# First stage of a two-layer streaming encoder: the third token block is scaled, shifted and split part by part

## The chip, the cores and the metric

The kernel runs on one core of a Trainium2 chip. The metric is the device time of one execution in microseconds (us), as the median over several executions. The core has a matrix engine (PE, with its weight loads listed as PEld), a vector engine (DVE), a scalar engine (ACT), a general engine (POOL) and a queue engine (SP) that issues most of the loads. Each engine works through its own queue of instructions in the order in which the program holds them; semaphores tie them together.

## The reference, cut to what matters

2,048 prompt tokens and 128 sample tokens (8 requests of 16) pass through two layers. Each layer normalises, modulates by a scale and a shift that depend on the request, mixes, and adds the result back. The change touches the beginning of the first layer only:

```
def rms_norm(x, g):
    xf = x.astype(F32)
    y = xf * lax.rsqrt(jnp.mean(xf * xf, axis=-1, keepdims=True) + EPS)
    return (y * g.astype(F32)).astype(x.dtype)
...
        h = rms_norm(x, norm_g[i]) * (1.0 + scale) + shift
...
    proj = h @ w_in
    u, z = jnp.split(proj, 2, axis=-1)
```

So `h = x * r * gs + shift`, where `r` is one number per token (the reciprocal root), `gs = norm_g * (1 + scale)` is one number per feature (and request), and `shift` likewise. All 2,048 prompt tokens share one request; the sample tokens have eight.

## The kernel before

**Layout.** The 2,176 tokens are cut into eight blocks, `j` = 0 to 7, of 272 tokens: 256 of the prompt (`NPC`) and 16 of the samples. A block is a tile `x` of 128 partitions by 8 by 272: feature `128 k + p` lies in part `k` on partition `p`. The program numbers blocks from 0, so the **third block** is `j` = 2; its tile is called `x2` here and shows as `x` in the profile.

**Products.** The products are done in three parts for accuracy. A block is split into a high part `hh` (what the matrix engine's 32-bit format holds) and a low part `hl` (the rest), each as two tiles of four parts (`_0` for k = 0 to 3, `_1` for k = 4 to 7); weights are split likewise (`wuh`, `wul`). `mm3` (L148 to L154) issues three matmuls for each k: high by high (L151), high weight by low block (L152), low weight by high block (L153). A column block `cb` of 128 outputs takes 24 matmuls into one accumulator tile `pd`, a token block takes 8 column blocks, 192 matmuls. From block 1 on four accumulator buffers serve `pd` in turn; ACT copies each finished one to `ev` and stores it to `u_d`.

**The first stage.** A loop over the blocks `j` does, in this order of the code: four column blocks; then the preparation of block `j + 1` (modulate and split), the load of `x` for block `j + 2`; then four more column blocks, and at the end (cb = 7) the normalisation `norm_x` of block `j + 2` (squares on ACT, sums on DVE, a sum over the partitions by two matmuls `ms`, a root on ACT, a reciprocal on DVE, and a multiply of the whole block by `r` on DVE). Block 0 and block 1 have code of their own ahead of the loop: block 0 is prepared k by k, and block 1 by `second_block`, part by part. Blocks 2 to 7 are prepared by `apply_mod` (L283), in three turns: eight activations on ACT that apply `gs` and the shift to the already normalised block in place, one after another (L291); a copy of four parts at a time to `hh` on ACT, and a subtraction on DVE for `hl` (`split_x`, L229). The modulated block is also stored to `h0_d[j]`, from where a later stage reads it again.

**What else runs on the engines there.** Small tables of the state-space mixer are made on DVE and POOL (`transitions`, `step_factors`, `s5_tables`, `rot_factors`, `rot_table`: the rows with `gk`, `sm`, `low`, `high`, `q`, `ca`, `cat`, `sp`, `tw`), and from block 2 on PE also does the products of `ada_steps` (`ada<-wa,cs`), whose weights SP loads between the blocks. The buffers of `x` are three, so the load of `x5` waits until `x2` is read and stored.

**What sets the order.** Each engine is wrapped in a class with a flag `ordered`. While it is set, that engine's instructions keep the order in which the code writes them (in the profile they all show the wrapper's line, L70). While it is not set, a scheduler chooses their places, and they show the line of the code that issues them. PE is ordered while `j` = 1; DVE and ACT are ordered while blocks 0 and 1 are prepared and while `x2` is normalised, and not after that.

**The later stages**, which the change does not touch: the scan of the state-space mixer with the product for `z` between its parts, the gating product (`pg`), the output product (`po`), the second layer's input product with its convolution (`pc`, `pz`), the sample tokens, and sixteen chunks of the delta rule with the last product (`epo`) beside them.

Of the kernel before, what the change touches and what calls it, by code (L numbers as in the profile page):

```python
# [10 lines left out]
F32 = mybir.dt.float32  # L11
F32R = mybir.dt.float32r
# [6 lines left out]
P = 128  # L19
# [3 lines left out]
NCH = 272  # L23
# [31 lines left out]
def kernel(ctx: ExitStack, tc: tile.TileContext, I, O, upto="Z"):  # L55
    nc = tc.nc
# [18 lines left out]
    T, V, S, G, SY = (Engine(e) for e in (nc.tensor, nc.vector, nc.scalar, nc.gpsimd, nc.sync))  # L75
# [10 lines left out]
    h0_d = [dr.tile([P, KC, NCH], F32, name=f"h0_d{i}") for i in range(8)]  # L86
# [133 lines left out]
    hp = pab.enter_context(tc.tile_pool(reuse_waits="tile", name="hp", bufs=4))  # L220
# [11 lines left out]
    with ExitStack() as pa:  # L232
        xp = pa.enter_context(tc.tile_pool(reuse_waits="tile", name="xp", bufs=3))
        sst = pa.enter_context(tc.tile_pool(reuse_waits="tile", name="sst", bufs=1))
# [12 lines left out]
        def norm_sq(xt, sqs=None, acc=None, part=range(2)):  # L247
            acc = sp1.tile([P, 2, NCH], F32, tag="acc", name="acc") if acc is None else acc
            for hf in part:
                sq = sqs[:, 4 * hf:4 * hf + 4] if sqs else sp1.tile([P, 4, NCH], F32, tag="sq", name="sq")  # L250
                xh = xt[:, 4 * hf:4 * hf + 4]
                S.activation(sq, xh, AF.Square)
                V.tensor_add(sq[:, 0:2], sq[:, 0:2], sq[:, 2:4])
                V.tensor_add(acc[:, hf], sq[:, 0], sq[:, 1])
            return acc
# [9 lines left out]
        def norm_r(acc, r=None, fold=False):  # L265
            ps = psn.tile([P, NCH], F32, tag="ms", name="ms")
            if fold:
                V.tensor_add(acc[:, 0], acc[:, 0], acc[:, 1])
            for hf in range(1 if fold else 2):
                T.matmul(ps, lhsT=onesd, rhs=acc[:, hf], start=(hf == 0), stop=(fold or hf == 1))  # L270
            r = sp1.tile([P, NCH], F32, tag="r", name="r") if r is None else r
            S.activation(r, ps, AF.Sqrt, bias=epst)
            V.reciprocal(r, r)
            return r
# [5 lines left out]
        def norm_x(xt, fold=False):  # L280
            return norm_mul(xt, norm_r(norm_sq(xt), fold=fold))

        def apply_mod(j, xt):  # L283
            xs = xt[:, :, NPC:NCH].rearrange("p k (q h) -> p k q h", h=2)
            V.tensor_mul(xs, xs, bc(gs0[:, :, 1:9], 3, 2))
            V.tensor_add(xs, xs, bc(modT[:, 0:8, 1:9], 3, 2))
            hl = []
            for hf in range(2):
                for k in range(4 * hf, 4 * hf + 4):
                    xk = xt[:, k, 0:NPC]  # L290
                    S.activation(xk, xk, AF.Identity, scale=gs0[:, k, 0:1], bias=modT[:, k, 0:1])  # L291
                hl.append(split_x(j, xt[:, 4 * hf:4 * hf + 4], hf))
            (h0, l0), (h1, l1) = hl
            if j < 7:
                nc.scalar.dma_start(h0_d[j], xt)
            return h0 + h1, l0 + l1

        def second_block(xt, r, copies):
            xs = xt[:, :, NPC:NCH].rearrange("p k (q h) -> p k q h", h=2)
            V.tensor_mul(xs, xs, bc(r[:, NPC:NCH].rearrange("p (q h) -> p q h", h=2), 1, KC))  # L300
            V.tensor_mul(xs, xs, bc(gs0[:, :, 1:9], 3, 2))
            V.tensor_add(xs, xs, bc(modT[:, 0:8, 1:9], 3, 2))
            a, b = ([hp.tile([P, 4, NCH], F32R, tag=t, name=f"{t}1_{hf}") for hf in range(2)] for t in ("hh", "hl"))
            for hf in range(2):
                for i in range(4):
                    k = 4 * hf + i
                    xk = xt[:, k, 0:NPC]
                    V.scalar_tensor_tensor(xk, r[:, 0:NPC], gs0[:, k, 0:1], xk, op0=ALU.mult, op1=ALU.mult)
                    S.activation(a[hf][:, i, 0:NPC], xk, AF.Identity, bias=modT[:, k, 0:1])
                S.copy(a[hf][:, :, NPC:NCH], xt[:, 4 * hf:4 * hf + 4, NPC:NCH])  # L310
                for cb in copies[hf]:
                    first_copy(cb)
                for i in range(4):
                    k = 4 * hf + i
                    V.scalar_tensor_tensor(b[hf][:, i, 0:NPC], xt[:, k, 0:NPC], modT[:, k, 0:1],
                                           a[hf][:, i, 0:NPC].bitcast(F32), op0=ALU.add, op1=ALU.subtract)
                V.tensor_sub(b[hf][:, :, NPC:NCH], xt[:, 4 * hf:4 * hf + 4, NPC:NCH],
                             a[hf][:, :, NPC:NCH].bitcast(F32))
            for k in range(KC):
                xk = xt[:, k, 0:NPC]  # L320
                S.activation(xk, xk, AF.Identity, bias=modT[:, k, 0:1])
            nc.scalar.dma_start(h0_d[1], xt)
            return [ks(t[0], 4) + ks(t[1], 4) for t in (a, b)]

        SY.ordered = True
# [74 lines left out]
        wt, raws = load_mod(0), [load_raw(0), load_raw(1)]  # L400
        T.ordered = V.ordered = S.ordered = True
        xsq = xp.tile([P, KC, NCH], F32, tag="x", name="xsq")
        r0 = norm_r(norm_sq(xcur, xsq), sst.tile([P, NCH], F32, name="r0"))
        W = 32
        sm = sst.tile([P, 11 * W], F32, name="sm")
        sml = [sm[:, i * W:(i + 1) * W] for i in range(11)]
# [1 line left out]
        for k in range(KC):  # L408
# [5 lines left out]
            if k == 6:  # L414
                xt1 = load_x(1)[0]
# [29 lines left out]
        for cb in range(6, 8):  # L445
            pd0 += [psd.tile([P, NCH], F32, tag="d", name=f"pd0_{cb}")]
            mm3(pd0[cb], ks(wu_hi[cb]), ks(wu_lo[cb]), *hcur)
        hnext = second_block(xt1, r1, ((2, 3), (4, 5)))
        first_copy(6)
        first_copy(7)  # L450
        after = [V.last]
# [169 lines left out]
        for j in range(8):  # L621
            hh, hl = hcur
            T.ordered = j == 1
            for cb in range(8):
                if cb == 4:
                    if j < 7:
                        hcur = apply_mod(j + 1, xnext) if j else hnext
                    V.ordered = S.ordered = j == 0
                    if j < 6:
                        xn, xl = load_x(j + 2)  # L630
                        if j == 0:
                            xnext = norm_x(xn)
                    V.ordered = S.ordered = False
                    SY.ordered = False
                    with later([i_] if j else after):
                        for part in TABLES.get(j, ()):
                            s5_tables(part)
                        if j == 1:
                            rot_factors()
                        for i in range(max(0, 3 * j - 3), min(3 * j, 16)):  # L640
                            rot_table(i)
                if j > 0:
                    ps = psd4.tile([P, NCH], F32, tag="d", name=f"pd{j}_{cb}")
                    i_ = mm3(ps, ks(wu_hi[cb]), ks(wu_lo[cb]), hh, hl)
                    store_u(j, cb, ps)
                if cb == 7 and 0 < j < 6:
                    xnext = norm_x(xn)
                if j > 1 and cb % 3 == 1:
                    with later([xl, i_]):
                        ada.pop(0)()  # L650
# [1666 lines left out]
```

## Time and profile before

| | |
|---|---|
| median of 3 executions | 2085.61 us (2085.01 to 2089.56) |
| the profiled execution | 2087.13 us, of which the span of the profile is 2085.4 us |
| granted PE clock, mean | 0.99 |
| VectorE (DVE) | 1476.3 us busy, 71% |
| ScalarE (ACT) | 1007.5 us busy, 48% |
| GpSimd (POOL) | 506.9 us busy, 24% |
| DMA | 343.74 MB, mean 165 GB/s |

The span is what the profiler saw from the first to the last instruction; 1.7 us of the execution lie around it. The engines work beside each other, so shares don't add to 100%. A share of the whole span says little about a change to one stage: the first stage is the first 260 us of the span, and block 2 is worked on in about 15 us of it. In rows of a timeline the first number is the start in us, the second the time from the first start to the last end of the row's instructions (`x4`: four of them), and brackets name how long the engine was idle before and what released it. Instructions of one engine overlap a little, so what one costs its engine is the distance from its start to the next one's start, which is called its step here. Rows of waits read: who waited for whom, us in total, how often, the longest.

### The profile page before, as it was taken

What the parts mean: (1) busy time and instruction counts of PE and PEld (TensorE: products, weight loads), DVE (VectorE), ACT (ScalarE), POOL (GpSimd) and SP (SyncE); (2) the same over time, 40 slices, a digit from 0 to 9 for tenths busy, and PEclk for the clock granted to TensorE, in tenths of its full rate; (3) what the DMA queues carried; (4) which work ended last, traced back from release to release, by engine and by line L of the source; (5) the groups of instructions that cost most, each with busy time, mean ns of one, the idle gap of its engine ahead of it and who ended that gap; (6) DMA issues with size and microseconds to landing.
All of it is one profiled execution on the core that took longest, in us unless ns stands there. A gap on an engine that the chain in (4) does not pass through costs nothing.

```text
span 2085.4 us, 41297 instructions
## 1 busy us (share of the span) xinstructions
PE 2042.6 (98%) x15473; PEld 1826.8 (88%) x15473; DVE 1476.3 (71%) x3401; ACT 1007.5 (48%) x2426; POOL 506.9 (24%) x759
## 2 busy tenths in 40 slices
PE   7999999999999999999999999999999899999998
PEld 5889988888899999999788979899987688888887
DVE  7989668777674455557565669688546878888885
ACT  4534445555454444446655322341224566666663
POOL 1268500000122222221100010110022544444430
PEclk8999999999999999999999999999999899999999
DMA  8797756666463333325565212653455834444532
GB/s 308 275 308 275 274 172 199 186 193 191 158 216 125 103 121 108 128 93 216 180 199 163 74 50 75 179 136 104 138 174 177 251 116 138 148 151 151 152 116 71
DMA packets 314611, 343.74 MB, mean 165 GB/s; under 512 B 88522, under 2 KB 261082, under 8 KB 311596
## 3 DMA queue, kind: packets, MB, share of 16 engines
q1 hardware_dynamic: 183196, 229.90, 35.2%
q10 hardware_dynamic: 125792, 94.38, 13.9%
q0 software_dynamic: 5424, 16.83, 2.2%
q8 instruction: 122, 2.00, 0.4%
q14 instruction: 77, 0.63, 0.1%
HBM read 220.81 MB, written 120.21 MB: 164 GB/s over the span
## 4 chain that ended last, share of the span: by engine, by line
PE 89%; DVE 4%; DMA 3%; ACT 3%; issue 1%; POOL 0%; SPq 0%; ACTq 0%; DVEq 0%; POOLq 0%
PE epo L70 9%; PE pdz L70 8%; PE pc L151 5%; PE pc L152 5%; PE pc L153 5%; PE pz L153 3%; PE pz L151 3%; PE pz L152 3%; PE py L70 3%; PE po L152 3%; PE po L153 3%; PE po L151 3%; PE pd L151 2%; PE pg L153 2%; PE pg L151 2%; PE pg L152 2%
## 5 line engine op out<-in xcount | busy, mean ns | idle before, releaser
L151 PE MATMUL pc<-h1h,wdh 128*128 128x512 f32 (+1 forms) x600 | 216.5, 361 | 0.8 <-ACT pb L1578 0.8
L152 PE MATMUL pc<-h1l,wdh 128*128 128x384 f32 (+1 forms) x600 | 214.9, 358 | 0.3 <-POOL h1l L1529 0.3
L153 PE MATMUL pc<-h1h,wdl 128*128 128x384 f32 (+1 forms) x600 | 215.0, 358 | 0.0
L1589 DVE SCALAR_TENSOR_TENSOR ac<-pb,convw,ac 128x384 f32<-128x384 f32 (+3 forms) x288 | 163.5, 591 | 3.3
L151 PE MATMUL po<-gh,woh 128*128 128x272 f32 x512 | 147.0, 290 | 1.6 <-ACT woh L137 1.5
L152 PE MATMUL po<-gl,woh 128*128 128x272 f32 x512 | 147.4, 289 | 0.9 <-DVE gl L1107 0.8
L153 PE MATMUL po<-gh,wol 128*128 128x272 f32 x512 | 148.0, 290 | 0.1
L70 PE MATMUL pdz<-hhz,wzh 128*128 128x272 f32 x448 | 131.0, 292 | 0.4 <-ACT evz L70 0.4
L152 PE MATMUL pg<-yl,wgh 128*128 128x272 f32 x448 | 129.9, 290 | 0.0
L151 PE MATMUL pg<-yh,wgh 128*128 128x272 f32 x448 | 129.3, 289 | 0.0
L70 PE MATMUL pdz<-hhz,wzl 128*128 128x272 f32 x448 | 129.2, 288 | 0.0
L153 PE MATMUL pg<-yh,wgl 128*128 128x272 f32 x448 | 129.2, 288 | 0.0
L70 PE MATMUL pdz<-hlz,wzh 128*128 128x272 f32 x448 | 128.8, 287 | 0.0
L151 PEld LDWEIGHTS pc<-h1h,wdh 128*128 128x128 f32 x600 | 112.7, 188 | 13.0 <-issue 1.7
L152 PEld LDWEIGHTS pc<-h1l,wdh 128*128 128x128 f32 x600 | 112.7, 188 | 10.6 <-issue 0.8
L153 PEld LDWEIGHTS pc<-h1h,wdl 128*128 128x128 f32 x600 | 112.7, 188 | 10.1 <-issue 0.8
L151 PE MATMUL pd<-hh,wuh 128*128 128x272 f32 x384 | 112.1, 294 | 2.8 <-ACT hh L229 2.8
L70 PE MATMUL epo<-w2h,ohi 128*128 128x512 f32 x272 | 111.7, 411 | 0.0
L153 PE MATMUL pd<-hh,wul 128*128 128x272 f32 x384 | 111.2, 290 | 0.0
L152 PE MATMUL pd<-hl,wuh 128*128 128x272 f32 x384 | 111.2, 290 | 0.0
L1104 POOL TENSOR_TENSOR zt<-zt,sz 128x272 f32<-128x272 f32 x64 | 61.3, 964 | 191.0 <-ACT sz L1103 187.9
L70 PE MATMUL epo<-w2h,olo 128*128 128x512 f32 x272 | 107.0, 393 | 0.0
(657 smaller groups left out, 6330.9 us busy)
## 6 DMA issues: line engine op xcount, KB each, us to landing
wa<-in_w_ada SPq DMA_DIRECT2D x32, 512.0 KB
wdr<-in_w_in SPq DMA_DIRECT2D x24, 512.0 KB
u_d<-ev ACTq DMA_DIRECT2D x64, 136.0 KB
u<-u_d SPq DMA_DIRECT2D x16, 544.0 KB
z_d<-evz ACTq DMA_DIRECT2D x64, 136.0 KB
y_d<-y ACTq DMA_DIRECT2D x32, 272.0 KB
zt<-z_d SPq DMA_DIRECT2D x64, 136.0 KB
xa<-in_xT SPq DMA_DIRECT2D x8, 1088.0 KB
```

The costliest lines, as they stand in the source:

```text
L70: i_ = f(*a, **kw)
L151: T.matmul(ps, lhsT=w_hi[k], rhs=x_hi[k], start=(k == 0), stop=False)
L152: T.matmul(ps, lhsT=w_hi[k], rhs=x_lo[k], start=False, stop=False)
L153: i_ = T.matmul(ps, lhsT=w_lo[k], rhs=x_hi[k], start=False, stop=(k == n - 1))
L1104: G.tensor_mul(zt, zt, sz)
L1589: V.scalar_tensor_tensor(o, src(j), convw[:, b, j:j + 1], o, op0=ALU.mult, op1=ALU.add)
```

## The change

`second_block` becomes `scaled_block(j, ...)` and is used for block 2 also. In the pass `j` = 0 of the loop, `x2` is no longer multiplied by `r`; only `r` itself is computed, into a tile of its own (`r2`, in the buffer that `r0` has left). In the pass `j` = 1, DVE and ACT are ordered while block 2 is prepared. Per part k, DVE multiplies the prompt tokens by `r` and `gs` in one instruction, ACT adds the shift and writes `hh` directly, and DVE adds the shift again and subtracts `hh`, which gives `hl`. The 16 sample tokens of all parts are done by three small instructions ahead, and copied and subtracted per half. What `apply_mod` left in `x2` for the store is made afterwards by eight activations, and the store to `h0_d[2]` follows them.

```diff
-        def second_block(xt, r, copies):
+        def scaled_block(j, xt, r, copies=((), ())):
             xs = xt[:, :, NPC:NCH].rearrange("p k (q h) -> p k q h", h=2)
             V.tensor_mul(xs, xs, bc(r[:, NPC:NCH].rearrange("p (q h) -> p q h", h=2), 1, KC))
             V.tensor_mul(xs, xs, bc(gs0[:, :, 1:9], 3, 2))
             V.tensor_add(xs, xs, bc(modT[:, 0:8, 1:9], 3, 2))
-            a, b = ([hp.tile([P, 4, NCH], F32R, tag=t, name=f"{t}1_{hf}") for hf in range(2)] for t in ("hh", "hl"))
+            a, b = ([hp.tile([P, 4, NCH], F32R, tag=t, name=f"{t}{j}_{hf}") for hf in range(2)] for t in ("hh", "hl"))
             for hf in range(2):
...
             for k in range(KC):
                 xk = xt[:, k, 0:NPC]
                 S.activation(xk, xk, AF.Identity, bias=modT[:, k, 0:1])
-            nc.scalar.dma_start(h0_d[1], xt)
+            nc.scalar.dma_start(h0_d[j], xt)
...
-        r0 = norm_r(norm_sq(xcur, xsq), sst.tile([P, NCH], F32, name="r0"))
+        r0 = norm_r(norm_sq(xcur, xsq), sst.tile([P, NCH], F32, tag="r0", name="r0"))
...
-        hnext = second_block(xt1, r1, ((2, 3), (4, 5)))
+        hnext = scaled_block(1, xt1, r1, ((2, 3), (4, 5)))
...
                     if j < 7:
-                        hcur = apply_mod(j + 1, xnext) if j else hnext
+                        if j == 1:
+                            V.ordered = S.ordered = True
+                        hcur = hnext if j == 0 else scaled_block(2, xt2, r2) if j == 1 else apply_mod(j + 1, xnext)
                     V.ordered = S.ordered = j == 0
                     if j < 6:
                         xn, xl = load_x(j + 2)
                         if j == 0:
-                            xnext = norm_x(xn)
+                            xt2, r2 = xn, norm_r(norm_sq(xn), sst.tile([P, NCH], F32, tag="r0", name="r2"))
```

Up to the point where `r` of block 2 is ready, the four compute engines hold the same instructions in the same order. The rows below are of the built programs: line, operation, output from inputs, and the waits that the instruction carries (on other engines, or on a DMA). `x_999` is block 2's tile.

On DVE, right after that reciprocal, the program of before holds the multiply of the whole block:

```order
L253 TENSOR_TENSOR sq<-sq 128x544 [waits Activation_49]
L70 TENSOR_TENSOR x_999<-x_999,r 128x2176 [waits DMAHW3_49,DVE_49]
L587 TENSOR_TENSOR cat_1601<-sp_1557 128x288 [waits DMASW5_49,DVE_49,Pool_49]
L502 TENSOR_TENSOR gk<-gk,sm 128x32 [waits DVE_49]
L503 TENSOR_TENSOR gk<-gk,sm 128x32
L254 TENSOR_TENSOR acc<-sq 128x272 [waits DVE_49]
L285 TENSOR_TENSOR x_999<-x_999,gs_186 128x8x16 [waits DVE_49]
L478 TENSOR_TENSOR q_1150<-low,gk 128x32x2 [waits DVE_49]
```

The changed program holds a multiply of the 128 sample values in that place, and table work around it as before:

```order
L253 TENSOR_TENSOR sq<-sq 128x544 [waits Activation_49]
L70 TENSOR_TENSOR x_999<-x_999,r_1010 128x8x16 [waits DMAHW3_49,DVE_49]
L587 TENSOR_TENSOR cat_1625<-sp_1581 128x288 [waits DMASW5_49,DVE_49,Pool_49]
L502 TENSOR_TENSOR gk<-gk,sm 128x32 [waits DVE_49]
L503 TENSOR_TENSOR gk<-gk,sm 128x32
L254 TENSOR_TENSOR acc<-sq 128x272 [waits DVE_49]
L70 TENSOR_TENSOR x_999<-x_999,gs_186 128x8x16 [waits DVE_49]
L478 TENSOR_TENSOR q_1174<-low,gk 128x32x2 [waits DVE_49]
```

Only the second row is another; the steps of the sample tokens have moved under the wrapper's line.

On DVE again, where the low part of block 2's first half is made. Before, one subtraction of four parts stands for it, late in the table work, and that of the second half (`hl_1`) ten rows after it:

```order
L502 TENSOR_TENSOR gk<-gk,sm 128x32 [waits DVE_49]
L503 TENSOR_TENSOR gk<-gk,sm 128x32
L229 TENSOR_TENSOR hl_0_1136<-x_999,hh_0_1135 128x1088 [waits Activation_49]
L589 TENSOR_TENSOR ca_1610<-ca_1610,cat_1611 128x288 [waits DVE_49]
L478 TENSOR_TENSOR q_1150<-low,gk 128x32x4 [waits DVE_49]
L273 RECIPROCAL r<-r 128x272 [waits Activation_49]
```

In the changed program the parts follow each other, with two table rows between the first and the other three of `hl_0`, and the first part of the second half's scaling behind them:

```order
L482 TENSOR_TENSOR q_1175<-low,gk 128x32x2
L70 SCALAR_TENSOR_TENSOR hl_0_1133<-x_999,modT,hh_0_1131 128x256 [waits Activation_49]
L587 TENSOR_TENSOR ca_1624<-sp_1581 128x288 [waits DMASW6_49,DMASW4_49,Pool_49]
L587 TENSOR_TENSOR ca_1624<-sp_1581 128x288
L70 SCALAR_TENSOR_TENSOR hl_0_1133<-x_999,modT,hh_0_1131 128x256 [waits Activation_49] x3
L70 TENSOR_TENSOR hl_0_1133<-x_999,hh_0_1131 128x4x16 [waits Activation_49]
L70 SCALAR_TENSOR_TENSOR x_999<-r_1010,gs_186,x_999 128x256
```

One instruction of 1,088 elements has become five, and the reciprocal of the next block, which stood behind `hl_0` and ahead of `hl_1`, still stands ahead of `hl_1`.

On PE, the start of block 2's products, right behind the last product of block 1. Before, four high products of `k` = 0 lead, then a sum `ms` of a later block, and then the low part is needed:

```order
L70 MATMUL ms<-acc,onesd 128x272 [waits DVE_49]
L151 MATMUL pd_0_1353<-hh_0_1135,wuh_219 128x272 [waits Activation_49]
L151 MATMUL pd_1_1381<-hh_0_1135,wuh_217 128x272
L151 MATMUL pd_2_1418<-hh_0_1135,wuh_215 128x272
L151 MATMUL pd_3_1446<-hh_0_1135,wuh_213 128x272
L270 MATMUL ms<-acc,onesd 128x272 [waits DVE_49,Activation_49]
L152 MATMUL pd_0_1353<-hl_0_1136,wuh_219 128x272 [waits DVE_49]
```

In the changed program the same four lead, and the low part follows at once:

```order
L70 MATMUL ms<-acc,onesd 128x272 [waits DVE_49]
L151 MATMUL pd_0_1377<-hh_0_1131,wuh_219 128x272 [waits Activation_49]
L151 MATMUL pd_1_1405<-hh_0_1131,wuh_217 128x272
L151 MATMUL pd_2_1442<-hh_0_1131,wuh_215 128x272
L151 MATMUL pd_3_1470<-hh_0_1131,wuh_213 128x272 [waits Activation_49]
L152 MATMUL pd_0_1377<-hl_0_1133,wuh_219 128x272 [waits DVE_49]
```

The sum `ms` has moved back; in the changed program it stands where the second half's low part is first needed, after 48 more products:

```order
L153 MATMUL pd_3_1470<-hh_0_1131,wul_214 128x272
L151 MATMUL pd_3_1470<-hh_1_1132,wuh_213 128x272
L270 MATMUL ms<-acc,onesd 128x272 [waits DVE_49]
L152 MATMUL pd_0_1377<-hl_1_1134,wuh_219 128x272 [waits DVE_49]
L153 MATMUL pd_0_1377<-hh_1_1132,wul_220 128x272
```

From the end of block 2 on, PE holds the same matmuls in the same order in both programs. On DVE, ACT, POOL and SP the scheduler has moved rows against each other up to the end of the first stage (the making of the tables above all), and a few among the sample tokens near the end of the kernel.

## The prediction

> **What bounds the kernel now.** I read the page first, for the engine that carries the time, then the waits of that engine, and then its timeline where it waited for what the change touches. The first row gives busy us, share of the span and instructions of the engines, the second the shares of the chain that ended last:
>
> ```profile
> PE 2042.6 (98%) x15473; PEld 1826.8 (88%) x15473; DVE 1476.3 (71%) x3401; ACT 1007.5 (48%) x2426; POOL 506.9 (24%) x759
> PE 89%; DVE 4%; DMA 3%; ACT 3%; issue 1%; POOL 0%; SPq 0%; ACTq 0%; DVEq 0%; POOLq 0%
> ```
>
> PE is the bound, so a change elsewhere pays only where PE stands still. The waits of PE name one such place in the change's reach (total, times, longest):
>
> ```profile
> PE pd L151 <- ACT hh L229: 2.8, 1, 2.8
> ```
>
> Now PE's timeline from the last products of block 1 (L70) to block 2 (L151 to L153):
>
> ```profile
> 85.01 0.29 PE L70 MATMUL pd<-hl,wuh 128*128 128x272 f32 x1
> ...
> 87.01 0.29 PE L70 MATMUL pd<-hh,wul 128*128 128x272 f32 x1
> 87.14 1.08 PE L70 MATMUL ms<-acc,onesd 128*128 128x272 f32 x4
> 91.00 0.77 PE L151 MATMUL pd<-hh,wuh 128*128 128x272 f32 x4 [2.78 <-ACT hh L229]
> 91.60 1.02 PE L270 MATMUL ms<-acc,onesd 128*128 128x272 f32 x2
> 92.36 0.59 PE L152 MATMUL pd<-hl,wuh 128*128 128x272 f32 x1
> ...
> 94.79 0.43 PE L153 MATMUL pd<-hh,wul 128*128 128x272 f32 x1
> 95.02 0.33 PE L152 MATMUL pd<-hl,wuh 128*128 128x272 f32 x1
> ```
>
> From 85.01 to 87.01 sixteen products start, 0.125 us apart. From 92.36 to 94.79 there are eleven, about 0.23 us apart. The granted clock says why; columns: stretch, length, then busy us and count for PE, PEld, DVE, ACT and POOL, granted PE clock, DMA share, GB/s:
>
> ```profile
> 63.00:64.00 1.00, 0.40 (x3) 0.31 (x3) 1.00 (x8) 1.00 (x4) 0.07 (x1) 1.00 0.90 295
> 92.00:93.00 1.00, 1.00 (x5) 0.64 (x4) 1.00 (x4) 1.00 (x2) 0.00 (x0) 0.50 0.95 374
> ```
>
> After the wait of 2.78 us the clock was 0.50 for some 3 us. The upper row is the start of block 1, where PE had two shorter waits, and the clock stayed 1.00. So the stall costs more than its idle time. Two sums `ms` cost 0.92 us at full clock:
>
> ```profile
> 147.88 0.92 PE ms L270 x4
> ```
>
> Block 2 could thus have started at 87.14 + 0.92 = 88.06. Up to 95.02 PE did 4 + 11 products and one `ms`, worth 15 x 0.125 + 0.46 = 2.34 us, and would have been there at 90.40. **The loss at this place is 95.02 - 90.40 = 4.62 us**, 0.22% of the execution, and the most that a better feed can win here.
>
> **What the wait hangs on.** PE waited for ACT's `hh` of the first half, made after the eight activations in turn:
>
> ```profile
> 84.33 0.39 ACT L332 COPY ev<-pd 128x272 f32<-128x272 f32 x1 [2.62 <-PE pd L70]
> ...
> 86.14 3.53 ACT L291 ACTIVATE x<-x,modT,gs 128x256 f32<-128x256 f32 x7
> ...
> 89.85 1.09 ACT L229 CAST hh<-x 128x1088 fp32r<-128x1088 f32 x1
> ```
>
> The change lets ACT write `hh` directly, from parts that DVE scales. So the question becomes when DVE delivers. DVE's steps from the multiply that goes (81.49) on:
>
> ```profile
> 81.49 2.41 DVE L70 TENSOR_TENSOR x<-x,r 128x2176 f32<-128x2176 f32 x1
> 83.82 0.45 DVE L587 TENSOR_TENSOR cat<-sp 128x288 f32<-128x288 f32 x1
> 84.19 0.18 DVE L502 TENSOR_TENSOR gk<-gk,sm 128x32 f32<-128x32 f32 x1
> ...
> 84.39 0.43 DVE L254 TENSOR_TENSOR acc<-sq 128x272 f32<-128x272 f32 x1
> 84.74 0.28 DVE L285 TENSOR_TENSOR x<-x,gs 128x128 f32<-128x128 f32 x1
> 84.94 0.22 DVE L478 TENSOR_TENSOR q<-low,gk 128x64 f32<-128x64 f32 x1
> ...
> 85.72 0.82 DVE L587 TENSOR_TENSOR ca<-sp 128x288 f32<-128x288 f32 x2
> 86.46 0.18 DVE L495 TENSOR_TENSOR gk<-sm 128x32 f32<-128x32 f32 x1
> ...
> 86.78 0.72 DVE L253 TENSOR_TENSOR sq<-sq 128x544 f32<-128x544 f32 x1
> 87.42 0.45 DVE L589 TENSOR_TENSOR ca<-ca,cat 128x288 f32<-128x288 f32 x1
> ...
> 92.80 1.84 DVE L273 RECIPROCAL r<-r 128x272 f32<-128x272 f32 x1
> 94.56 0.12 DVE L492 TENSOR_TENSOR sm<-gk 128x32 f32<-128x32 f32 x1
> ```
>
> Steps: the big multiply 2.33, a table row of 288 0.37, the sum of squares 0.64 and its second add 0.35, a sample row 0.20, the reciprocal 1.76, a small table row 0.09 to 0.14. The new kinds stand in block 1, which is prepared in the new way already:
>
> ```profile
> 60.25 1.67 DVE L70 SCALAR_TENSOR_TENSOR x<-r,gs,x 128x256 f32<-128x256 f32 x4
> 61.84 1.67 DVE L70 SCALAR_TENSOR_TENSOR hl<-x,modT,hh 128x256 fp32r<-128x256 f32 x4
> 63.42 0.21 DVE L70 TENSOR_TENSOR hl<-x,hh 128x64 fp32r<-128x64 f32 x1
> 63.56 0.18 DVE L511 COPY gk<-un 128x64 f32<-128x64 f32 x1
> ```
>
> Four scaling parts take 1.59 us, 0.40 each; so do four low parts; the samples' low part 0.14.
>
> **The change, part by part.** DVE reaches the changed row at 81.49 as before. Up to the end of `hl_0` its order then holds, for block 2, three sample rows (0.60), four scalings and four low parts (3.20) and the samples' low part (0.14): 3.94 us. Between them stand three rows of 288 (1.11), one 0.35, one 0.64 and fourteen small rows (1.57): 3.67 us. `hl_0` is done at 81.49 + 7.61 = 89.10, plus 0.07 by which the last row outlasts its step: **89.17**. Up to the end of `hl_1` come eight more parts and a sample row (3.34), three rows of 288 (1.11), one 0.35, the reciprocal (1.76) and three small rows (0.33): 6.89 us. **`hl_1` is done at 96.06.** DVE has no idle time in that stretch of the trace; the waits in its new order are for table stores issued long before, and for ACT.
>
> ACT costs nothing here. A part takes it (shortest, median and longest, in ns, of block 1's eight):
>
> ```profile
> L70 ACT ACTIVATE hh<-x,modT x8: 493/494/511, 57.5 to 62.0; 128x256 fp32r<-128x256 f32 x8
> ```
>
> After its copy at 84.33 it finds DVE's first parts waiting and makes four by 86.4, well before 88.06. Those of the second half follow DVE's scalings, which end near 90.9, and PE asks for them only after 38 more products.
>
> PE, then: the four leading products from 88.06 to 88.56; a wait for `hl_0` until 89.17 plus the hand-over of 0.06 (63.63 to 63.69 in block 1) = 89.23, **0.67 us**. The first product after such a wait took 0.23 us instead of 0.125:
>
> ```profile
> 63.69 0.40 PE L70 MATMUL pd<-hl,wuh 128*128 128x272 f32 x1 [0.60 <-DVE hl L70]
> 63.92 0.29 PE L70 MATMUL pd<-hh,wul 128*128 128x272 f32 x1
> ```
>
> So 48 products and `ms` end at 89.23 + 0.10 + 6.00 + 0.46 = 95.79, and `hl_1` comes at 96.12: another wait of **0.33 us**, and 0.10 again. Block 2 then runs from 96.22 what it could have run from 88.06 + 52 x 0.125 + 0.46 = 95.02. **The loss left is 1.20 us, the gain 4.62 - 1.20 = 3.42 us.** The bounds: no loss left (gain 4.62), and both waits plus the half clock again, whose price in before was 4.62 - 2.94 (91.00 less 88.06) = 1.68 us (gain 1.74).
>
> [...]
>
> What is moved, and covered. The eight identities for the store are off every path to PE, but the store of block 2 waits for them, and the load of `x5` into its buffer for the store; that load, on SP's queue, would be issued some 5 us later:
>
> ```profile
> 97.32 0.33 SPq L244 DMA_DIRECT2D x<-in_xT  x1
> 102.88 8.52 SPq L181 DMA_DIRECT2D wa<-in_w_ada  x4
> ```
>
> SP's queue stood still for 5.2 us behind it anyway, until the next `wa` load could go, and the first reader of `x5` is a square for the norm of block 5, three blocks ahead of PE: cost nothing, and without that cover at most the same 5 us on one product of `ada`. DVE gets 0.60 + 6.40 + 0.28 = 7.28 us of work for 2.33 + 0.40 + 2 x 1.20 = 5.13, so it runs 2.15 us later, while PE runs 3.4 us earlier. Next late would be block 3's low part:
>
> ```profile
> 108.94 1.28 DVE L229 TENSOR_TENSOR hl<-x,hh 128x1088 fp32r<-128x1088 f32 x1
> ...
> 121.23 0.32 PE pd L151
> ```
>
> It ended at 110.2, and PE asked at about 121.2; 11.0 - 2.15 - 3.42 = 5.4 us of cover remain. If that were gone, each further us would cost a us. After block 2 no wait of PE for DVE or ACT shows until the stage ends, so the gain should reach the end.
>
> **Rivals.**
> - *The feed gets ahead of PE* (table rows take less, or DVE starts sooner): both waits vanish at 0.7 us less on DVE, gain 4.6, 2081.0 us. For it: the fourteen small rows and the handovers carry my walk; against it: DVE was never idle there.
> - *The half clock returns* although the waits are short: 1.68 more, gain 1.7, 2083.9. For it: one case of a fall below 3 us; against it: block 1.
> - *The gain is given back later*, at a place that DMA or DVE sets (3% and 4% of the chain), or through the moved table rows: 2085.6. Against it: those pieces start from what PE has finished.
> - *DVE becomes the bound: slower.* Five rows stand for one, and each pays its start: 256 elements take 0.40 of step where 1,088 took 1.20. If the 2.15 us of extra work land on `hl_1` (a handover per part, say), it comes at 98.27, the second wait is 2.48 us, about what halved the clock, and the loss is 0.77 + 2.48 + 1.68 = 4.93: 0.3 us slower than before, 2085.9, and each further us costs one. It decides from 1.8 us on. Against it: all of that extra work is already in my walk.
>
> [...]
>
> The order of the built program shows the parts in place, so that nothing changes is no case.
>
> **How the numbers follow.** The profiled execution took 2087.13 us (span 2085.4), and becomes 2083.7; it lies 1.5 us above the median shown, 2085.61, from which the same gain gives **2082.2 us**. Chances: forecast 0.52, feed ahead 0.22, half clock 0.12, given back 0.06, DVE bound 0.08. About 0.2% (4.2 us) is what a measurement of this kernel can tell from no change. Beyond it lie the feed-ahead case and 0.06 of the forecast's spread: faster 0.28. Slower by as much needs DVE 6 us late, or an accident of the moved rows: 0.06. Same: 0.66. The range runs from 2080.0 (feed ahead and a little luck with the clock later) to 2086.0 (given back, DVE bound).
>
> **What would show it.** Right: PE's wait for `hh` at block 2 gone, two waits for `hl` below 1 us each, the clock at 1.00 from 88 to 97, `hl_0` near 89.2 and `hl_1` near 96.1, and block 3 starting 3.4 us earlier. Wrong: a second wait above 2 us, a stretch at 0.50, a new wait of PE between 97 and 260 us, or an earlier block 3 without an earlier end.

## The result, and the profile after

| | before | after | ratio, 95% interval |
|---|---|---|---|
| with the prediction's result, 13 runs each | 2087.73 us | 2082.79 us (2079.20 to 2084.63) | 0.998 (0.9973 to 0.9987) |
| the changed kernel once more, 35 and 11 runs | 2086.51 us | 2082.36 us (2080.22 to 2084.81) | 0.9979 (0.997 to 0.9987) |

The ratios are a gain of 4.2 and 4.4 us, with intervals of 2.7 to 5.6 and 2.7 to 6.3 us. The forecast was 2082.2 us and a gain of 3.42 us. PE is the bound as before; busy time, then the shares of the chain:

```profile
PE 2041.0 (98%) x15473; PEld 1824.8 (88%) x15473; DVE 1477.0 (71%) x3417; ACT 1011.3 (49%) x2434; POOL 513.9 (25%) x759
PE 88%; DVE 5%; DMA 3%; ACT 2%; issue 1%; POOL 0%; SPq 0%; ACTq 0%; DVEq 0%
```

The wait of 2.8 us for `hh` is gone from PE's waits; between 86 and 100 us one row is left:

```profile
PE pd L152 <- DVE hl L70: 0.5, 1, 0.5
```

PE's timeline at block 2 of the changed kernel (start, length, row, idle before and its releaser):

```profile
86.43 1.08 PE L70 MATMUL ms<-acc,onesd 128*128 128x272 f32 x4
87.15 0.86 PE L151 MATMUL pd<-hh,wuh 128*128 128x272 f32 x4
88.49 0.39 PE L152 MATMUL pd<-hl,wuh 128*128 128x272 f32 x1 [0.48 <-DVE hl L70]
88.72 0.29 PE L153 MATMUL pd<-hh,wul 128*128 128x272 f32 x1
...
94.61 0.62 PE L270 MATMUL ms<-acc,onesd 128*128 128x272 f32 x2
95.28 0.39 PE L152 MATMUL pd<-hl,wuh 128*128 128x272 f32 x1
95.51 0.29 PE L153 MATMUL pd<-hh,wul 128*128 128x272 f32 x1
```

The four leading products follow the sums at once. The first product with `hl` waits until 88.49. After that the steps are 0.125 us again, until the first product of the second half at 95.28. The windows (columns as in the prediction) have the clock at 1.00 where PE waited, and so it is in each microsecond from 88 to 97:

```profile
88.00:89.00 1.00, 0.52 (x5) 0.51 (x5) 1.00 (x5) 0.17 (x2) 0.00 (x0) 1.00 0.33 106
95.00:96.00 1.00, 0.96 (x7) 0.72 (x6) 1.00 (x4) 0.64 (x2) 0.00 (x0) 1.00 0.00 0
```

DVE's rows for block 2, from the changed row to the last row of `hl_1`:

```profile
80.76 0.29 DVE L70 TENSOR_TENSOR x<-x,r 128x128 f32<-128x128 f32 x1
...
88.21 0.23 DVE L70 TENSOR_TENSOR hl<-x,hh 128x64 fp32r<-128x64 f32 x1
...
91.62 1.86 DVE L273 RECIPROCAL r<-r 128x272 f32<-128x272 f32 x1
...
93.42 1.67 DVE L70 SCALAR_TENSOR_TENSOR hl<-x,modT,hh 128x256 fp32r<-128x256 f32 x4
94.99 0.23 DVE L70 TENSOR_TENSOR hl<-x,hh 128x64 fp32r<-128x64 f32 x1
```

How far the gain carries is read from the chain of waits. In before, the next four-fold `ms` stood at 147.88; after:

```profile
115.48 0.46 PE ms L270 x2
143.58 0.92 PE ms L270 x4
```

From the first `ms` behind block 1 (87.14, 86.43) to that row, before took 60.74 us and after takes **57.15 us: 3.59 us less**. This stretch is called the place below. The next stage begins with the first product `pdz`, before and after:

```profile
260.66 0.37 PE L70 MATMUL pdz<-hh,wzh 128*128 128x272 f32 x1
```

```profile
256.36 0.37 PE L70 MATMUL pdz<-hh,wzh 128*128 128x272 f32 x1
```

From the first `ms` to `pdz` that is 173.52 and 169.93 us, again 3.59 us apart: nothing is given back in the stage. The span of the two profiles, though, differs by 7.9 us (2085.4 and 2077.5). Of the other 4.3, 0.71 lie ahead of the first `ms`, where the two programs hold the same instructions, and 3.6 behind `pdz`, in stages that the change does not touch (1824.7 and 1821.1 us). Whether these are the change's is the first question for a run.

### The profile page after: what moved, and what is told of

It reads as the page before. It is cut to its first block, busy times and chain, and to the rows that moved or that the text cites. A ratio compares the mean times of both kernels' runs of the same rounds, so it can differ in the third digit from the quotient of the medians.

```text
span 2077.5 us, 41322 instructions
## 1 busy us (share of the span) xinstructions
PE 2041.0 (98%) x15473; PEld 1824.8 (88%) x15473; DVE 1477.0 (71%) x3417; ACT 1011.3 (49%) x2434; POOL 513.9 (25%) x759
## 4 chain that ended last, share of the span: by engine, by line
PE 88%; DVE 5%; DMA 3%; ACT 2%; issue 1%; POOL 0%; SPq 0%; ACTq 0%; DVEq 0%
PE epo L70 9%; PE pdz L70 8%; PE pc L151 5%; PE pc L152 5%; PE pc L153 5%; PE po L153 3%; PE po L152 3%; PE pz L153 3%; PE po L151 3%; PE pz L151 3%; PE pz L152 3%; PE py L70 3%; PE pg L153 2%; PE pg L151 2%; PE pg L152 2%; PE pd L151 2%
## 5 line engine op out<-in xcount | busy, mean ns | idle before, releaser
L152 PEld LDWEIGHTS pc<-h1l,wdh 128*128 128x128 f32 x600 | 112.7, 188 | 10.4 <-issue 0.8
L153 PEld LDWEIGHTS pc<-h1h,wdl 128*128 128x128 f32 x600 | 112.6, 188 | 10.2 <-issue 0.8
```

The source lines that it names most:

```text
L152: T.matmul(ps, lhsT=w_hi[k], rhs=x_lo[k], start=False, stop=False)
L153: i_ = T.matmul(ps, lhsT=w_lo[k], rhs=x_hi[k], start=False, stop=(k == n - 1))
```

## Experiments

All use the same two readings: the place (in the expectations its end is read from the chain, as here; the timeline's row starts 0.16 us earlier), and the stretch from the first `ms` to the first `pdz`. The best possible place is 60.74 less the 4.62 us of the prediction, 56.12 us.

| run | place, us | to `pdz`, us | gain to `pdz` | gain by the ratio of the runs (interval) |
|---|---|---|---|---|
| before | 60.74 | 173.52 | | |
| after | 57.15 | 169.93 | 3.59 | 4.2 (2.7 to 5.6) |
| e1_same | 57.17 | 169.95 | 3.57 | 4.4 (2.7 to 6.3) |
| e2_order | 60.54 | 173.32 | 0.20 | 0.0 (-1.7 to 1.7) |
| e3_split | 56.31 | 169.09 | 4.43 | 3.8 (2.1 to 5.6) |
| e4_hl1_late | 60.88 | 173.66 | -0.14 | -0.2 (-1.9 to 1.7) |
| e5_hl1_half | 58.27 | 171.05 | 2.47 | 2.9 (1.0 to 4.8) |
| e6_samples_first | 56.87 | 169.65 | 3.87 | 5.2 (3.5 to 7.1) |
| e7_samples_last | 62.04 | 175.17 | -1.65 | -0.6 (-2.7 to 1.3) |
| e8_recip | 56.88 | 172.08 | 1.44 | 2.7 (-0.2 to 5.4) |
| e9_all | 57.19 | 174.82 | -1.30 | -12.9 (-15.4 to -10.4) |
| e10_grain | 57.83 | 170.61 | 2.91 | 3.1 (1.3 to 5.0) |

The last column is what the ratio of the runs leaves of 2087 us. But for e9_all, each interval holds the gain up to `pdz`, so the runs speak for what is won or lost there reaching the end; the intervals are 2.9 us wide or more and cannot show it to the microsecond. Each place is read from one profiled execution; e1_same says how well such a reading repeats (57.15 and 57.17).

**e1_same: the changed kernel once more.**

> The changed kernel once more, beside the kernel before. The place is measured from PE's first sum `ms` behind block 1 to the row of four sums `ms` near 145 us: 60.74 us in the profile of before (87.14 to 147.88), 57.15 in that of the changed kernel (86.43 to 143.58). Theory A (the forecast's sum, all of the gain lies at block 2): again 57.1 to 57.2 at the place, and a median 3.0 to 4.2 us below that of before. Theory B (the change also moves something later, since the medians lay 4.9 us apart): the same 57.15 at the place, but 4.5 us or more in the median, and a stage behind the first one that is again shorter by a microsecond or more.

Place 57.17, span 2081.1. From `pdz` (256.67) to the end it took 1824.4 us, as before did (1824.7); the eleven profiles other than e9_all's lie between 1821.1 and 1825.6, and next to the lowest, with 1821.7, stands e7_samples_last, which is slower at block 2. So the 3.6 us behind `pdz` in the first profile of the changed kernel are that execution's own, and theory B has no stage to stand on. The median lies 4.15 us below before; the interval holds the place's 3.57, and the difference can't be resolved.

**e2_order: the order without the parts** (an edit of before).

```diff
+                        V.ordered = S.ordered = j == 1
                         hcur = apply_mod(j + 1, xnext) if j else hnext
```

> The order alone: the kernel before, with DVE and ACT held to the order of the code while block 2 is prepared (root multiply, eight activations and copies as before, but the copy `hh_0` behind four activations and not eight). By the rows of before: `hh_0` done at 88.8, so PE waits 0.8 us at 88.06; `hl_0` stands behind the same table rows as before up to 89.83 and takes 1.28, done 91.1, a second wait of 1.8 us; `hl_1` at about 95.9, before PE asks. Theory A (what counts is when `hl_0` is ready, and two waits below 2 us leave the clock at 1.00): the end of block 2's first column blocks is 2.7 us late instead of 4.6, so 58.8 us at the place, and a median about 1.9 us below before. Rival 1 (the order is the whole of the change's gain): 57.2. Rival 2 (the clock falls for two waits so close together): 60.4, no gain.

Place 60.54: rival 2. On PE, ACT and DVE:

```profile
89.84 0.76 PE L151 MATMUL pd<-hh,wuh 128*128 128x272 f32 x4 [0.81 <-ACT hh L70]
92.19 0.72 PE L270 MATMUL ms<-acc,onesd 128*128 128x272 f32 x2 [1.59 <-ACT r L272]
```

```profile
89.69 2.08 ACT L70 ACTIVATE x<-x,modT,gs 128x256 f32<-128x256 f32 x4
91.67 0.47 ACT L272 ACTIVATE r<-ms,epst 128x272 f32<-128x272 f32 x1
```

```profile
90.53 1.28 DVE L70 TENSOR_TENSOR hl<-x,hh 128x1088 fp32r<-128x1088 f32 x1
```

The first wait is as forecast. `hl_0` was done at 91.81, but PE had a sum `ms` next, whose buffer ACT had to free by the root at 91.67, queued behind four activations. After the two waits, 2.4 us together, the clock fell to 0.50 (at 93.1, for 3.4 us), though each of them is below 2 us. Whether it took both waits, this run does not show.

**e3_split: the parts without the order** (an edit of the changed kernel, as all below but e10_grain).

```diff
                         if j == 1:
-                            V.ordered = S.ordered = True
+                            V.ordered = S.ordered = False
```

> The parts alone: the changed kernel without the two flags that hold DVE and ACT to the order of the code at block 2; the scheduler then puts the second half's four scalings and three rows of 288 ahead of the last part of `hl_0`. Walk of DVE in the changed kernel's profile from 80.76: three sample rows 0.60, eight scalings 3.20, four low parts 1.60, two samples' low parts 0.28, five rows of 288 1.85, 0.35, 0.64, fifteen small rows 1.65, together 10.2 us, so `hl_0` is done at 91.0. PE is there at 87.85: a wait of 3.1 us. Theory A (order and parts are needed together): the clock falls as in before, loss 3.1 + 0.1 + 1.7 = 4.9 us, 61.0 at the place, a median like that of before or slightly above. If the clock stays at 1.00: 59.4. Rival (the parts are what gains, whatever the order): 57.2.

Place 56.31, and no wait of PE for block 2 at all: theory A is wrong, the rival is right, and the place is better still than its 57.2. On PE and on DVE:

```profile
87.59 1.08 PE L70 MATMUL ms<-acc,onesd 128*128 128x272 f32 x4
88.31 0.86 PE L151 MATMUL pd<-hh,wuh 128*128 128x272 f32 x4
89.07 0.39 PE L152 MATMUL pd<-hl,wuh 128*128 128x272 f32 x1
```

```profile
83.83 0.48 DVE L315 SCALAR_TENSOR_TENSOR hl<-x,modT,hh 128x256 fp32r<-128x256 f32 x1
...
88.81 0.21 DVE L317 TENSOR_TENSOR hl<-x,hh 128x64 fp32r<-128x64 f32 x1
...
90.08 0.47 DVE L315 SCALAR_TENSOR_TENSOR hl<-x,modT,hh 128x256 fp32r<-128x256 f32 x1
...
91.72 0.87 DVE L315 SCALAR_TENSOR_TENSOR hl<-x,modT,hh 128x256 fp32r<-128x256 f32 x2
```

The last part of `hl_0` is the first of the two rows at 91.72 and was ready at about 92.2, 10.2 us behind the row at 81.97 with which the samples' rows begin: the walk was right. PE did not wait for it: it began at 89.07, when only the part of k = 0 and the samples' small row (88.81 to 89.02) were there. That this row came just as PE was ready (its last leading product began near 88.9) is luck. The built programs say why one part was enough. PE is not held to the order of the code at block 2, so the scheduler chooses. PE's rows behind the four leading products (names shortened: `pd2_1` is block 2's column block 1), in the changed kernel:

```
L152 MATMUL pd2_0<-hl2_0,wuh0 [waits DVE]
L153 MATMUL pd2_0<-hh2_0,wul0
L151 MATMUL pd2_0<-hh2_0,wuh0
L152 MATMUL pd2_0<-hl2_0,wuh0
...
```

and in e3_split:

```
L152 MATMUL pd2_0<-hl2_0,wuh0 [waits DVE]
L153 MATMUL pd2_0<-hh2_0,wul0
L151 MATMUL pd2_0<-hh2_0,wuh0
L152 MATMUL pd2_1<-hl2_0,wuh1
...
```

In the changed kernel the samples' row is the last of `hl_0`, every product needs its columns, so the half is ready in one moment, and PE's program works off one column block after another. In e3_split the samples' row stands ahead of three of the parts, and PE's program turns over four column blocks for each k: 12 products, 1.5 us, for each part that costs DVE 0.40. This is theory C, which e6_samples_first and e7_samples_last test from both sides.

**e4_hl1_late and e5_hl1_half: DVE made late for the second half.**

```diff
+        pad = sst.tile([P, 8], F32, name="pad")
...
+                if j == 2 and hf == 1:
+                    V.tensor_reduce(pad, bc(r[:, 0:NPC], 1, 8), axis=mybir.AxisListType.X, op=ALU.add)
                 for i in range(4):
```

Both eights are fours in the second.

> The rival that DVE becomes the bound, forced: the changed kernel with one more instruction on DVE between the second half's scalings and `hl_1`, a sum over 8 times 256 elements that nothing reads. By the multiply of 2,176 elements (2.33 us) it takes about 2.2 us. Then `hl_1` comes at 97.4 where PE asks at 95.07: a wait of 2.3 us. If the clock falls, as after the wait of 2.78 us in before: 57.15 + 2.2 + 1.7 = 61.0 at the place, 0.3 us slower than before (the rival's price in the prediction). If it stays at 1.00 after 2.3 us: 59.3, still 1.4 us faster than before. A third way, that PE works on other products meanwhile: 57.2.

> The delay of `hl_1` halved: the same added sum on DVE over 4 times 256 elements, by the 2.28 us that 8 times 256 took about 1.15 us. With 2.28 us PE stood still twice within 3 us for 2.0 us together, the clock was 0.50 from 99.1 on for 3.3 us, and the place took 60.72 us. Now PE should stand still for about 1.0 us. If the clock falls only from some 2 us of idle on: 58.2 to 58.4 at the place, clock 1.00 throughout. If any second wait after the first brings the half clock: 59.8 to 60.0.

The sum took 2.28 us in e4_hl1_late, which came to 60.88 at the place: the rival's price (61.0) to 0.1 us. PE, and the windows that follow:

```profile
96.98 0.72 PE L270 MATMUL ms<-acc,onesd 128*128 128x272 f32 x2 [0.89 <-DVE acc L254]
98.78 0.39 PE L152 MATMUL pd<-hl,wuh 128*128 128x272 f32 x1 [1.07 <-DVE hl L70]
```

```profile
99.00:100.00 1.00, 1.00 (x6) 1.00 (x6) 1.00 (x2) 0.67 (x2) 0.00 (x0) 0.54 0.00 0
102.00:103.00 1.00, 1.00 (x8) 1.00 (x7) 1.00 (x5) 0.60 (x1) 0.07 (x1) 0.75 0.98 400
```

With half the delay, 58.27, as expected: one wait of 1.07 us at the second half, the clock at 1.00, and the delay is paid one for one: the first product of the second half came 9.97 us behind the first `ms` (96.31 less 86.34; 8.85 in the changed kernel), 1.12 us later, and the place is 1.12 us above the changed kernel's.

**e6_samples_first and e7_samples_last: the samples' row ahead, order kept; and behind, order free.**

```diff
+                if j == 2:
+                    V.tensor_sub(b[hf][:, :, NPC:NCH], xt[:, 4 * hf:4 * hf + 4, NPC:NCH],
+                                 a[hf][:, :, NPC:NCH].bitcast(F32))
                 for i in range(4):
...
-                V.tensor_sub(b[hf][:, :, NPC:NCH], xt[:, 4 * hf:4 * hf + 4, NPC:NCH],
-                             a[hf][:, :, NPC:NCH].bitcast(F32))
+                if j == 1:
+                    V.tensor_sub(b[hf][:, :, NPC:NCH], xt[:, 4 * hf:4 * hf + 4, NPC:NCH],
+                                 a[hf][:, :, NPC:NCH].bitcast(F32))
```

```diff
-                    V.scalar_tensor_tensor(b[hf][:, i, 0:NPC], xt[:, k, 0:NPC], modT[:, k, 0:1],
-                                           a[hf][:, i, 0:NPC].bitcast(F32), op0=ALU.add, op1=ALU.subtract)
-                V.tensor_sub(b[hf][:, :, NPC:NCH], xt[:, 4 * hf:4 * hf + 4, NPC:NCH],
-                             a[hf][:, :, NPC:NCH].bitcast(F32))
+                    low = V.scalar_tensor_tensor(b[hf][:, i, 0:NPC], xt[:, k, 0:NPC], modT[:, k, 0:1],
+                                                 a[hf][:, i, 0:NPC].bitcast(F32), op0=ALU.add, op1=ALU.subtract).ins
+                with later([low]):
+                    V.tensor_sub(b[hf][:, :, NPC:NCH], xt[:, 4 * hf:4 * hf + 4, NPC:NCH],
+                                 a[hf][:, :, NPC:NCH].bitcast(F32))
...
-                            V.ordered = S.ordered = True
+                            V.ordered = S.ordered = False
```

> The changed kernel, order kept, but the samples' small low part of each half stands ahead of its four low parts instead of behind them. Theory C (new, from the parts alone: a product needs the low part of its own k and the samples' low part; with the samples last, all of `hl_0` is one unit and PE takes one column block after the other; with the samples first PE's program turns over four column blocks per k, 12 products or 1.5 us for each part of 0.40 us): PE waits neither at 87.85, where the first part is there at 87.3, nor later in the first half; at the second half 0 to 0.4 us. The place: 56.2 to 56.7 us (best possible 56.12, the kernel after 57.15). Rival (it was the freedom of the scheduler on DVE and ACT that took the waits away): 57.1.

> The parts alone again (no order held), but with the samples' low part of each half tied behind its four low parts. By the rows of the parts-alone run, with the first `ms` at 87.59, `hl_0` is then complete at about 92.4, while PE would be ready at 89.0. Theory C: the first half is one unit again, PE waits 3.4 us, the clock falls, the loss is 3.4 + 0.1 + 1.7 = 5.2 us, 61.3 at the place, slower than before by 0.6 us. Rival (parts alone win wherever the samples stand, since PE has other products to do): 56.2 to 56.5, as in the parts-alone run (56.15).

PE in e6_samples_first, where the first product with `hl` follows without a wait, and the second half waits once:

```profile
87.81 0.86 PE L151 MATMUL pd<-hh,wuh 128*128 128x272 f32 x4
88.53 0.39 PE L152 MATMUL pd<-hl,wuh 128*128 128x272 f32 x1
...
95.67 0.39 PE L152 MATMUL pd<-hl,wuh 128*128 128x272 f32 x1 [0.39 <-DVE hl L70]
```

and in e7_samples_last, with two windows of its clock:

```profile
91.12 0.60 PE L152 MATMUL pd<-hl,wuh 128*128 128x272 f32 x1 [2.92 <-DVE hl L318]
```

```profile
90.00:91.00 1.00, 0.00 (x0) 0.00 (x0) 1.00 (x5) 0.51 (x3) 0.00 (x0) 0.75 0.00 0
97.00:98.00 1.00, 1.00 (x8) 1.00 (x8) 1.00 (x1) 0.00 (x0) 0.00 (x0) 0.84 0.98 409
```

Theory C holds on both sides. Moving one row of 0.14 us ahead takes the first wait away with the order kept. Moving it behind, without the order, brings a wait of 2.9 us and, in its profile, a slower place than before's; its runs can't be told from before's. The built programs agree: e6_samples_first holds PE's order of e3_split, four column blocks in turn, and e7_samples_last that of the changed kernel, one column block after another. Two sizes were off: e6_samples_first came to 56.87, not 56.2 to 56.7, since its second half still waits behind the next block's reciprocal (95.67 less 94.66 and 0.46, 0.55 us by the steps); e7_samples_last to 62.04, not 61.3, since the clock stayed at 0.50 for twice as long (last section).

**e8_recip: the next block's reciprocal behind `hl_1`.**

```diff
...
-            V.reciprocal(r, r)
+            with later(after):
+                V.reciprocal(r, r)
...
-                    xnext = norm_x(xn)
+                    xnext = norm_x(xn, after=[low2] if j == 1 else ())
```

where `low2` is the last row of `hl_1`, handed on from `norm_x` to `norm_r`.

> The changed kernel with the next block's reciprocal (1.76 us) placed behind `hl_1` instead of ahead of it. The forecast's walk: `hl_1` comes 1.76 us earlier, the second wait (about 0.2 us and 0.10 of restart) goes, the first (0.48 and 0.10) stays: 56.8 to 56.9 at the place, 0.3 us better, too little for the median. If the reciprocal now comes too late for block 3: a new wait of PE near 107 us, and more than 57.2.

Place 56.88, as the walk says. But to `pdz` it is 172.08 in this profile, 2.1 us worse than the changed kernel. PE, and DVE ahead of the copy `mA` that PE waited for:

```profile
258.88 0.86 PE L195 MATMUL adaT<-ident,mA 128*128 128x128 f32 x4 [2.10 <-DVE mA L192]
```

```profile
253.69 0.46 DVE L588 TENSOR_TENSOR cat<-sp 128x288 f32<-128x288 f32 x1 [1.93 <-POOL sp L484]
...
258.14 0.68 DVE L192 COPY mA<-ada 128x512 f32<-128x512 f32 x1
```

The same two rows in the changed kernel:

```profile
247.55 0.46 DVE L587 TENSOR_TENSOR cat<-sp 128x288 f32<-128x288 f32 x1 [1.37 <-POOL sp L483]
...
252.23 0.69 DVE L192 COPY mA<-ada 128x512 f32<-128x512 f32 x1
```

The order on DVE just ahead of `mA` is the same in both programs, and both wait for POOL there. Counted from the first `ms`, `mA` came 5.0 us later in e8_recip (170.83 against 165.80). The scheduler has moved table rows on DVE and POOL earlier in the stage, which is the mechanism of the prediction's rival "the gain is given back later, through the moved table rows"; that it was these rows that made `mA` late was not traced. Nor do the runs show the loss: the median of the eleven executions is 2082.46 us, as good as the changed kernel's, the profiled one took 2084.76, and two took 2091.47 and 2091.68.

**e9_all: blocks 3 to 7 part by part as well.**

```diff
...
-                        if j == 1:
+                        if j:
                             V.ordered = S.ordered = True
-                        hcur = hnext if j == 0 else scaled_block(2, xt2, r2) if j == 1 else apply_mod(j + 1, xnext)
+                        hcur = hnext if j == 0 else scaled_block(j + 1, xt2, r2)
...
-                    xnext = norm_x(xn)
+                    xt2, r2 = xn, norm_r(norm_sq(xn))
```

> Blocks 3 to 7 prepared part by part as well (root folded into the scaling, DVE and ACT held to the order of the code at each). Theory A (the change pays only where PE stands still, and before the end of the stage it does so at block 2 alone): 57.15 us at the place, and from the sums `ms` near 145 us to the first product `pdz` 112.94 us as in before (147.72 to 260.66) and after (143.42 to 256.36); the ratio to before about 0.998, as for the kernel after. Rival 1 (parts are better everywhere): below 112.5. Rival 2 (some 2 us more of DVE's time per block, and the order held across table work, cost somewhere): above 113.5, and a new wait of PE for `hl` or for a transposed sum.

Rival 2: the place is unchanged, 117.8 us from there to `pdz` instead of 112.9, and a ratio of 1.0062 (1.005 to 1.0074). The larger part comes behind `pdz`, in PE's waits there:

```profile
PE abT L70 <- DVE abt L735: 10.6, 3, 6.0
PE adaT L195 <- DVE mA L192: 3.1, 1, 3.1
```

DVE's rows that the next stage needs came late; before has neither of these waits. Which of the two did it, the added DVE time or the held order, was not separated.

**e10_grain: parts of the copy and the subtraction alone** (an edit of before).

```diff
+                    if j == 2:
...
+                        S.copy(a[:, k - 4 * hf], xt[:, k])
+                        V.tensor_sub(b[:, k - 4 * hf], xt[:, k], a[:, k - 4 * hf].bitcast(F32))
...
-                        hcur = apply_mod(j + 1, xnext) if j else hnext
+                        S.ordered = j == 1
+                        hcur = apply_mod(j + 1, xnext) if j else hnext
```

> The kernel before, with one edit: at block 2 the copy to `hh` and the subtraction for `hl` are done per part of 272 elements instead of per half, and ACT is held to the order activation, copy, activation, copy. The root multiply of 2,176 elements, the eight activations in place and the samples' rows stay; nothing is folded. Theory C (what counts is that a product waits for its own part only, 1.5 us of products per part): by before's rows ACT gives a part per 0.9 us from 84.6 on, the first `hl` part is there at about 88, no wait above 0.5 us, clock 1.00: 56.2 to 56.8 at the place, a ratio of 0.997 to 0.9985. Rival (the gain needs the root folded into the scaling, so that `hh` comes early): PE waits for `hh` or `hl` between 88 and 92 for 1 us or more, 57.5 to 60.7.

57.83: the time lies in the rival's bracket, but the rival's sign, a wait of 1 us or more, is missing (the longest is 0.54 us). So neither account is right as it stands. The wait at the start of block 2 is gone and the clock stays at 1.00, without folding the root into the scaling; the parts with ACT's order are worth 2.91 us to `pdz`. What is lost against e3_split is one part of `hl_0` that stands behind the reciprocal, on DVE and PE:

```profile
90.30 1.84 DVE L273 RECIPROCAL r<-r 128x272 f32<-128x272 f32 x1
92.06 0.38 DVE L296 TENSOR_TENSOR hl<-x,hh 128x272 fp32r<-128x272 f32 x1
```

```profile
92.49 0.39 PE L152 MATMUL pd<-hl,wuh 128*128 128x272 f32 x1 [0.54 <-DVE hl L296]
```

and a wait of 0.42 us for a copy `ev` at 103.46. The rest of the difference was not traced.

## Why the prediction was right, point by point

- **The loss of 4.62 us.** e3_split, in which PE waits for nothing at block 2, gains 4.43 of them.
- **DVE's walk.** Forecast from the changed row to the end of `hl_0` 7.68 us, to the end of `hl_1` 14.57. Measured 88.44 - 80.76 = 7.68 and 95.22 - 80.76 = 14.46.
- **The waits.** Forecast 0.67 and 0.33 us. By the same arithmetic the first is 88.49 less (86.43 + 0.92 + 0.50), 0.64 us (the profile counts 0.48 of it as idle), the second 95.28 - 95.07 = 0.21. The loss left was to be 1.20 and is 57.15 - 56.12 = 1.03; the gain was to be 3.42 and is 3.59.
- **The clock** stayed at 1.00 (each window from 88 to 97 us), as forecast. At block 1 of before, too, it was at 1.00 in each window from 61 to 67 us, with waits of 0.67 (at 62.70) and 0.60 us. The price of the half clock is right too: e4_hl1_late, the forecast's last rival made to happen, lands 0.1 us from the price expected of it. That rival spoke of one wait of 2.48 us; in e4_hl1_late the delay came as two waits, 0.89 and 1.07 us, and the clock fell all the same.
- **The cover.** The step that failed is "so it runs 2.15 us later": DVE's next root multiply began 15.37 us behind the changed row (96.13) where it had been 15.72 (97.21), because table rows moved behind it. The cover of block 3's `hl` became 7.7 us (109.16 to 116.87), not 5.4. The load of `x5` went out at 99.82, 3.2 us later against the first `ms`, not 5. Neither entered the sum.
- **The cost of small instructions**, the mechanism of the forecast's last rival, did not decide. The cost is there: the five rows of `hl_1` took 1.71 us (93.42 to 95.13) where one row took 1.20 (96.01 to 97.21). But the changed kernel, e3_split and e6_samples_first win 3.6 to 4.4 us up to `pdz` all the same. DVE's busy time over the whole run can't show such a cost: it was 1476.3 us before and 1477.0 us in the changed kernel.
- **The median.** The gain was set against 2085.61, the median of three runs. The medians of before in the later comparisons were 2086.47 to 2087.73. So the 0.6 us between forecast and result flatter it: a base that was 2.1 us too low and a difference of the medians of 4.9 us, where 3.4 were forecast, nearly cancel. That is luck; the 3.59 us at the place are not. The forecast also held some 0.2% to be the least that a measurement of this kernel can tell from no change. The intervals are finer: that of the 13 runs, 0.9973 to 0.9987, lies clear of 1.
- **What the forecast did not see.** It took each half of `hl` for one unit, as it is in the changed kernel, and put the wait that is left on DVE's time. The runs show that the unit is made by the place of one small row, and that the order, which it counted as part of the change, is worth 0.20 us alone (e2_order), while the parts without it gain 4.43. The rival "the feed gets ahead" was thus open without any saving on DVE.

No version beats the changed kernel beyond the noise: e3_split and e6_samples_first are 0.84 and 0.28 us shorter up to `pdz`, and the intervals of their ratios overlap with its own.

## What to carry to other kernels

Where the bounding engine waits for a block, ask what its first instruction needs, not when the block is complete: a feed in parts works if each part gives the consumer more work than the next part costs the producer (here 1.5 us against 0.40), and if no small row shared by all parts stands last. An edit in a program that a scheduler orders moves rows far behind it, and in one execution more was lost 160 us later than was gained on the spot (e8_recip), so follow it to the end of the stage, and ask the runs whether the loss is more than that execution's. What helps at the one block where PE stands still can harm at those where it does not (e9_all, ratio 1.0062).

## What the runs showed of the hardware

At block 2 the clock was at 0.50 for 3.4 us, in one run for twice that. Adding up twice the missing clock of the windows: in before 0.32 + 3.00 + 0.10 = 3.4 us (0.84, three windows at 0.50, 0.95), in e4_hl1_late 0.92 + 2.00 + 0.50 = 3.4 us, in e7_samples_last 0.50 + 6.00 + 0.32 = 6.8 us. In e7_samples_last the fall came at 90.5, while PE still waited, and not, as in before (91.68), e2_order (93.1) and e4_hl1_late (99.1), after its restart. Why it lasted twice as long there the runs do not say.

In the profile of before the clock was also at 0.50 from 16.59 to 30.24 us, and in the first profile of the changed kernel from 15.25 to 28.91: 13.65 us in both, 1.34 us apart, though the compute engines hold the same instructions up to there. After that it was at 1.00 until 91.68 in before, and until 598.93 in the changed kernel. So the place of a kernel whose clock falls, before's too, holds what one execution met; how much it differs between executions was not measured.

No single length of a wait parts the falls from the rest. The clock fell after one wait of 2.78 us (before) and during one of 2.92 us (e7_samples_last), but also after two of 0.81 and 1.59 us (e2_order) and after two of 0.89 and 1.07 us (e4_hl1_late). It stayed at 1.00 after one of 0.48 us in the changed kernel and after one of 1.07 us in e5_hl1_half, as long as the longest in e4_hl1_late. What decides, the runs do not say.
